# A matrix product with layer norm on one core: four row blocks worked on together over halves of B, another load order, and extra matmuls on zeros

## The chip, the cores and the metric

One Trainium2 chip, of which the kernel uses one core. The metric is the device time in microseconds of one execution. The engines of the core run side by side: TensorE (matmuls and transposes), VectorE, ScalarE, POOL (here it issues the loads) and SyncE (here it issues the stores). The profile names them PE (PEld for TensorE's weight loads), DVE, ACT, POOL and SP.

## The reference

```python
def reference(a, b, gamma, beta, eps):       # a, b: 2048 x 2048 float32
    x = np.matmul(a, b)
    mean = np.mean(x, axis=-1, keepdims=True)
    var = np.var(x, axis=-1, keepdims=True)
    normalized = (x - mean) / np.sqrt(var + eps)
    return (gamma * normalized + beta).astype(np.float32)
```

A row of the product can be normalised only when all of its 2048 columns are there. gamma, beta and eps are inputs like a and b; eps is a plain number.

## The kernel before, in words

**Tiles.** The 2048 rows of A are 16 row blocks of 128 (index `i`, later `p`). The contraction has 16 k tiles of 128 (`kt`). The 2048 columns of the result are four quarters of 512 (`q`); one quarter of a row block fills one PSUM bank. There are eight banks: seven for results (`cps`, line 110) and one for transposes (`tps`, line 74).

**Loads.** POOL issues all loads, which also turn float32 into float16. A row block of A (`emit_a_load`, line 62) is one transfer: 1 MB read, 512 KB written. B is loaded once and stays (`b16`): one transfer per k tile over all 2048 columns (line 95), of the same size. The order on the queue is A 0, A 1, B 0 to 15, A 2, A 3, gamma, beta (lines 81 to 99); later blocks of A follow inside the main loop (line 176), each after a buffer has come free (four buffers, line 47).

**Transposes.** TensorE needs A with the contraction on the partitions. `emit_transposes` (line 70) makes, per row block, two halves of eight 128 x 128 transposes into the one `tps` bank; ScalarE copies each half to `at` (line 78) before the next half may be written.

**Main loop (line 159).** For each row block, for each k tile, four matmuls (one per quarter, `emit_mm`, line 113) add into four banks. The transposes of the next row block stand in the middle. In the last row block the quarters run one after the other. When a quarter is complete, `quarter_done` (line 122) measures it (`bn_stats`, VectorE) and copies it to SBUF (`x`, ScalarE), which frees its bank. `emit_ln_stats` makes mean and 1/sqrt(var + eps); `emit_ln_stt` does the two passes of VectorE over each quarter (`u`, line 147, and `c`, line 151), and SyncE stores half a row block at a time (line 157), the last row block in quarters.

**What sets the order.** The order in the program text is a priority. A planner with its own cost model lays out every engine's queue, and an instruction that it deems ready can be put ahead of one that stands earlier in the text. So in the trace the matmuls of row block 1 are mixed with those of row block 0 while B comes in, until the seven banks are taken. All buffers' waits are put in by the framework. Engines work their queues in order.

Of the kernel before, what the change touches and what calls it, by code (L numbers as in the profile page):

```python
# [10 lines left out]
FP16 = mybir.dt.float16  # L11
AluOp = mybir.AluOpType
# [3 lines left out]
@with_exitstack  # L16
def kernel(
    ctx: ExitStack,
    tc: tile.TileContext,
    a: bass.AP,  # L20
    b: bass.AP,
    gamma: bass.AP,
    beta: bass.AP,
    eps: bass.AP,
    out: bass.AP,
):
    nc = tc.nc
    P = 128
    M, K = a.shape
    K2, N = b.shape  # L30
    assert K == K2
    assert M % P == 0 and K % P == 0 and N % 2048 == 0
    n_mt = M // P
    n_kt = K // P
    NB = 512
    n_nb = N // NB

    if isinstance(eps, bass.AP):
        eps_ap = eps
        eps_val = None  # L40
    else:
        eps_ap = None
        eps_val = float(eps)

    konst = ctx.enter_context(tc.tile_pool(name="konst", bufs=1))
    bpool = ctx.enter_context(tc.tile_pool(name="bpool", bufs=1))
    a16p = ctx.enter_context(tc.tile_pool(name="a16p", bufs=4))
    atp = ctx.enter_context(tc.tile_pool(name="atp", bufs=3))
    xpool = ctx.enter_context(tc.tile_pool(name="xpool", bufs=8))
    upool = ctx.enter_context(tc.tile_pool(name="upool", bufs=4))  # L50
    cpool = ctx.enter_context(tc.tile_pool(name="cpool", bufs=2))
    stat = ctx.enter_context(tc.tile_pool(name="stat", bufs=4))
    psum = ctx.enter_context(tc.tile_pool(name="psum", bufs=1, space=bass.MemoryType.PSUM))

    gamma_b = konst.tile([P, N], FP32)
    beta_b = konst.tile([P, N], FP32)
    eps_t = konst.tile([P, 1], FP32)
    ident = konst.tile([P, P], FP16)

    b16 = bpool.tile([P, n_kt, N], FP16)  # L60

    def emit_a_load(i):
        a16 = a16p.tile([P, K], FP16, tag="a16", name=f"a16_{i}")
        nc.gpsimd.dma_start(a16, a[ts(i, P), :])  # L64
        return a16

    a16_lst = [None] * (n_mt + 2)
    at_lst = [None] * (n_mt + 1)

    def emit_transposes(i):  # L70
        a16 = a16_lst[i]
        at = atp.tile([P, n_kt, P], FP16, tag="at", name=f"at{i}")
        for h in range(2):
            t_ps = psum.tile([P, n_kt // 2, P], FP16, tag="tps", bufs=1,
                             name=f"tps{i}_{h}")
            for j in range(n_kt // 2):
                nc.tensor.transpose(t_ps[:, j, :], a16[:, ts(h * 8 + j, P)], ident)  # L77
            nc.scalar.copy(at[:, ds(h * 8, 8), :], t_ps)  # L78
        return at

    a16_lst[0] = emit_a_load(0)
    a16_lst[1] = emit_a_load(1)
    nc.vector.memset(ident, 0.0)  # L83
    nc.gpsimd.affine_select(  # L84
        out=ident, in_=ident, compare_op=AluOp.not_equal, fill=1.0,
        base=0, pattern=[[-1, P]], channel_multiplier=1,
    )
    if eps_ap is not None:
        nc.sync.dma_start(eps_t, eps_ap.unsqueeze(0).to_broadcast([P, 1]))
    else:  # L90
        nc.vector.memset(eps_t, eps_val)
    at_lst[0] = emit_transposes(0)
    at_lst[1] = emit_transposes(1)
    for kt in range(n_kt):
        nc.gpsimd.dma_start(b16[:, kt, :], b[ts(kt, P), :])  # L95
    a16_lst[2] = emit_a_load(2)
    a16_lst[3] = emit_a_load(3)
    nc.gpsimd.dma_start(gamma_b, gamma.unsqueeze(0).to_broadcast([P, N]))  # L98
    nc.gpsimd.dma_start(beta_b, beta.unsqueeze(0).to_broadcast([P, N]))  # L99

    bnst_l = [None] * n_mt
    c_ps_l = [[None] * n_nb for _ in range(n_mt)]
    x_sb_l = [[None] * n_nb for _ in range(n_mt)]
    rstd_l = [None] * n_mt
    mv_l = [None] * n_mt

    def alloc_q(i, q):
        if bnst_l[i] is None:
            bnst_l[i] = stat.tile([P, n_nb, 6], FP32, tag="bnst", name=f"bnst{i}")
        c_ps_l[i][q] = psum.tile([P, NB], FP32, tag="c_ps", bufs=7,  # L110
                                 name=f"cps_{i}_{q}")

    def emit_mm(i, q, kt):
        nc.tensor.matmul(  # L114
            c_ps_l[i][q],
            at_lst[i][:, kt, :],
            b16[:, kt, ds(q * NB, NB)],
            start=(kt == 0),
            stop=(kt == n_kt - 1),
        )  # L120

    def quarter_done(i, q):
        nc.vector.bn_stats(bnst_l[i][:, q, :], c_ps_l[i][q])  # L123
        x_sb = xpool.tile([P, NB], FP32, tag="x_sb", name=f"x_{i}_{q}")
        nc.scalar.copy(x_sb, c_ps_l[i][q])  # L125
        x_sb_l[i][q] = x_sb

    def emit_ln_stats(i):
        mv = stat.tile([P, 2], FP32, name=f"mv{i}")
        nc.vector.bn_aggr(mv, bnst_l[i])  # L130
        ve = stat.tile([P, 1], FP32, name=f"ve{i}")
        nc.vector.tensor_tensor(ve, mv[:, 1:2], eps_t, AluOp.add)  # L132
        sq = stat.tile([P, 1], FP32, name=f"sq{i}")
        nc.scalar.activation(sq, ve, ActFn.Sqrt)  # L134
        rstd = stat.tile([P, 1], FP32, name=f"rstd{i}")
        nc.vector.reciprocal(rstd, sq)  # L136
        mv_l[i] = mv
        rstd_l[i] = rstd

    def emit_ln_stt(i, split_out=2):  # L140
        mv, rstd = mv_l[i], rstd_l[i]
        c_sb = cpool.tile([P, N], FP32, tag="c_sb", name=f"c{i}")
        nq_per_out = n_nb // split_out
        for q in range(n_nb):
            qs = ds(q * NB, NB)
            u = upool.tile([P, NB], FP32, tag="u", name=f"u_{i}_{q}")
            nc.vector.scalar_tensor_tensor(  # L147
                u, x_sb_l[i][q], mv[:, 0:1], gamma_b[:, qs],
                AluOp.subtract, AluOp.mult,
            )  # L150
            nc.vector.scalar_tensor_tensor(  # L151
                c_sb[:, qs], u, rstd, beta_b[:, qs],
                AluOp.mult, AluOp.add,
            )
            if (q + 1) % nq_per_out == 0:
                o = ds((q + 1 - nq_per_out) * NB, nq_per_out * NB)
                nc.sync.dma_start(out[ts(i, P), o], c_sb[:, o])

    for i in range(n_mt):
        last = i == n_mt - 1  # L160
        for q in range(n_nb):
            alloc_q(i, q)
        if last:
            for q in range(n_nb):
                for kt in range(n_kt):
                    emit_mm(i, q, kt)
                quarter_done(i, q)
        else:
            for kt in range(n_kt):
                for q in range(n_nb):  # L170
                    emit_mm(i, q, kt)
                if kt == n_kt // 2 - 1:
                    if i + 1 >= 3 and i + 1 < n_mt:
                        at_lst[i + 1] = emit_transposes(i + 1)
                    if i + 4 < n_mt:
                        a16_lst[i + 4] = emit_a_load(i + 4)
            for q in range(n_nb):
                if i == 1 and q == 1:
                    at_lst[2] = emit_transposes(2)
                quarter_done(i, q)  # L180
        emit_ln_stats(i)
        if i == 1:
            emit_ln_stt(0)
            emit_ln_stt(1)
        elif i >= 2:
            emit_ln_stt(i, split_out=(2 if not last else 4))


# [33 lines left out]
```

## Time and profile before

| what | us |
|---|---|
| median of four runs (279.56 to 279.72) | 279.65 |
| the profiled execution, whole | 279.64 |
| its span, first to last instruction | 277.6 |
| TensorE matmul and transpose busy | 245.2 |
| VectorE busy | 132.7 |
| ScalarE busy | 74.0 |
| POOL busy | 18.6 |

The span is measured between instructions, so it is shorter than the execution's own time. TensorE's instructions are pipelined: one that is listed with 381 ns may start 0.22 us after the one before it, so the pace is read from the starts of a run of them, and "busy" counts the union of their times. An instruction's line is that of the kernel's text above; several instructions of one line in a row are merged into one row with their count. A wait is put down to what came last by the profile.

### The profile page before, as it was taken

The page shows a single profiled execution, that of the slowest core. Times are in us where ns is not written, and L with a number is a line of the kernel's source. Part 1 is how long each engine was busy: PE and PEld are TensorE (multiplying, and loading weights), DVE is VectorE, ACT ScalarE, POOL GpSimd, SP SyncE. Part 2 cuts the span into 40 slices and gives each one's busy share as a digit, 9 for nine tenths or more (in the row PEclk, how much of TensorE's full clock was granted, in tenths as well). Part 3 has the DMA queues.
Part 4 walks back from the last instruction along what each step waited for, and adds up shares of the span by engine and source line. Part 5 has one row for each costly group of instructions (what it writes and reads, how often), then busy time and mean ns, then how long its engine had stood idle before and what let it go on. Part 6 is the DMA issues. An engine that isn't in the chain of part 4 may idle for free.

```text
span 277.6 us, 3149 instructions
## 1 busy us (share of the span) xinstructions
PE 245.2 (88%) x1280; PEld 116.2 (42%) x1280; DVE 132.7 (48%) x242; ACT 74.0 (27%) x114; POOL 18.6 (7%) x39
## 2 busy tenths in 40 slices
PE   0597657989999999999999999999999999999940
PEld 0252222445454444445454545454444545454410
DVE  0000000489663829091837456372909192745754
ACT  1220000562322222232323232222223232323110
POOL 7222211000000000000000000000000000000000
PEclk9999999999999999999999999999999999999995
DMA  6999999998734251616061433425111203030304
GB/s 114 212 213 212 214 216 210 308 272 235 217 151 78 100 128 76 153 44 178 8 188 39 162 67 151 76 113 116 76 76 64 91 0 153 0 151 2 151 0 151
DMA packets 9805, 35.84 MB, mean 129 GB/s; under 512 B 1088, under 2 KB 1088, under 8 KB 9536
## 3 DMA queue, kind: packets, MB, share of 16 engines
q0 software_dynamic: 4896, 18.88, 33.7%
q1 hardware_dynamic: 4896, 16.78, 15.2%
q8 instruction: 10, 0.16, 0.3%
q14 instruction: 3, 0.02, 0.0%
HBM read 35.65 MB, written 16.78 MB: 189 GB/s over the span
## 4 chain that ended last, share of the span: by engine, by line
PE 78%; DMA 17%; DVE 2%; issue 1%; ACT 1%; DVEq 0%; POOL 0%; ACTq 0%; POOLq 0%
PE cps L114 72%; DMA b<-in_b_dram 14%; PE tps L77 5%; DMA a<-in_a_dram 3%; DVE u L147 1%; ACT at L78 1%; DVE c L151 1%; DVE bnst L123 0%; DVEq L217 0%; POOL a L64 0%; DVE mv L130 0%; DVE ve L132 0%; DVE rstd L136 0%; ACTq L78 0%; POOLq L203 0%
## 5 line engine op out<-in xcount | busy, mean ns | idle before, releaser
L114 PE MATMUL cps<-b,at 128*128 128x512 f16 x1024 | 231.6, 381 | 12.8 <-DMA b<-in_b_dram 12.8
L114 PEld LDWEIGHTS <-at 128*128 128x128 f16 x1024 | 99.3, 98 | 130.5 <-issue 20.4
L123 DVE BATCH_NORM_STATS2 bnst<-cps 128x6 f32<-128x512 f32 x64 | 40.1, 687 | 135.2 <-PE cps L114 135.2
L125 ACT COPY x<-cps 128x512 f32<-128x512 f32 x64 | 37.5, 587 | 106.9 <-DVE bnst L123 106.1
L78 ACT COPY at<-tps 128x1024 f16<-128x1024 f16 x32 | 32.4, 1012 | 86.6 <-PE tps L77 86.6
L147 DVE SCALAR_TENSOR_TENSOR u<-x,mv,gamma_b 128x512 f32<-128x512 f32 x64 | 46.0, 743 | 2.2 <-DMA gamma_b<-in_gamma_dram 2.2
L151 DVE SCALAR_TENSOR_TENSOR c<-u,rstd,beta_b 128x512 f32<-128x512 f32 x64 | 45.2, 747 | 0.0
L77 PE MATMUL tps<-ident,a 128*128 128x128 f16 x256 | 21.1, 230 | 9.0 <-DMA a<-in_a_dram 6.5
L77 PEld LDWEIGHTS <-a 128*128 128x128 f16 x256 | 18.2, 103 | 19.8 <-issue 8.4
L64 POOL DMA_DIRECT2D a<-in_a_dram x16 | 8.6, 537 | 145.8 <-PE tps L77 137.6
L95 POOL DMA_DIRECT2D b<-in_b_dram x16 | 8.5, 542 | 18.1 <-DMA b<-in_b_dram 15.4
L130 DVE BATCH_NORM_AGGREGATE mv<-bnst 128x2 f32<-128x24 f32 x16 | 4.2, 264 | 0.5
L134 ACT ACTIVATE sq<-ve 128x1 f32<-128x1 f32 x16 | 3.3, 206 | 0.2 <-DVE ve L132 0.2
L136 DVE RECIPROCAL rstd<-sq 128x1 f32<-128x1 f32 x16 | 2.5, 158 | 1.7 <-ACT sq L134 1.7
L132 DVE TENSOR_TENSOR ve<-mv,eps_t 128x1 f32<-128x1 f32 x16 | 2.5, 159 | 0.5
L78 ACT ACT_TABLE_LOAD x1 | 1.3, 1283 | 0.7 <-PEq L203 0.7
L134 ACT ACT_TABLE_LOAD x1 | 1.3, 1283 | 0.0
L99 POOL DMA_DIRECT2D beta_b<-in_beta_dram x1 | 0.5, 527 | 3.5 <-DMA b<-in_b_dram 3.5
L98 POOL DMA_DIRECT2D gamma_b<-in_gamma_dram x1 | 0.5, 527 | 1.9 <-DMA b<-in_b_dram 1.9
L83 DVE MEMSET ident<- 128x64 uint32 x1 | 0.1, 112 | 0.8 <-PEq L203 0.8
L84 POOL TENSOR_SCALAR_AFFINE_SELECT ident<-ident 128x128 f16<-128x128 f16 x1 | 0.3, 312 | 0.1
L203 POOL MEMSET const-float32-0.0<- 128x1 f32 x1 | 0.1, 99 | 0.2 <-issue 0.2
(4 smaller groups left out, 0.4 us busy)
## 6 DMA issues: line engine op xcount, KB each, us to landing
out_dram<-c SPq DMA_DIRECT2D x30, 512.0 KB, 2.6
a<-in_a_dram POOLq DMA_DIRECT2D x16, 512.0 KB, 5.2
b<-in_b_dram POOLq DMA_DIRECT2D x16, 512.0 KB, 19.4
gamma_b<-in_gamma_dram POOLq DMA_DIRECT2D x1, 1024.0 KB, 20.3
beta_b<-in_beta_dram POOLq DMA_DIRECT2D x1, 1024.0 KB, 18.8
out_dram<-c SPq DMA_DIRECT2D x4, 256.0 KB, 2.6
```

The source lines that it names most:

```text
L64: nc.gpsimd.dma_start(a16, a[ts(i, P), :])
L77: nc.tensor.transpose(t_ps[:, j, :], a16[:, ts(h * 8 + j, P)], ident)
L78: nc.scalar.copy(at[:, ds(h * 8, 8), :], t_ps)
L95: nc.gpsimd.dma_start(b16[:, kt, :], b[ts(kt, P), :])
L114: nc.tensor.matmul(c_ps_l[i][q], at_lst[i][:, kt, :], b16[:, kt, ds(q * NB, NB)], start=(kt == 0), stop=(kt == n_kt - 1),)
L123: nc.vector.bn_stats(bnst_l[i][:, q, :], c_ps_l[i][q])
L125: nc.scalar.copy(x_sb, c_ps_l[i][q])
L130: nc.vector.bn_aggr(mv, bnst_l[i])
L132: nc.vector.tensor_tensor(ve, mv[:, 1:2], eps_t, AluOp.add)
L134: nc.scalar.activation(sq, ve, ActFn.Sqrt)
L147: nc.vector.scalar_tensor_tensor(u, x_sb_l[i][q], mv[:, 0:1], gamma_b[:, qs], AluOp.subtract, AluOp.mult,)
L151: nc.vector.scalar_tensor_tensor(c_sb[:, qs], u, rstd, beta_b[:, qs], AluOp.mult, AluOp.add,)
```

## The change

Four row blocks (0 to 3) are now worked on together. B is loaded in halves of its columns: first, for every k tile, columns 0 to 1023 (quarters 0 and 1), then for every k tile columns 1024 to 2047. On the first halves TensorE adds into seven quarters at once: (0,0), (0,1), (1,0), (1,1), (2,0), (2,1), (3,0), the list `L7`; then (3,1) alone; then quarters 2 and 3 of row blocks 0 and 1, and then those of 2 and 3. Row blocks 4 to 15 run as before.

On the load queue, row block 0 of A comes in two halves, blocks 1 to 3 stand between the first half tiles of B, and all later blocks are issued behind gamma and beta, each waiting for a free buffer. The transposes of row blocks 4 and 5 stand in the stage of row blocks 2 and 3, and later ones are made two row blocks ahead instead of one. There are six `at` buffers instead of three and 20 `x` buffers instead of eight.

The order of TensorE's instructions in the first stage (up to (3,1)) is written out by hand and kept by `manual_schedule`. In it stand 29 extra matmuls on a tile of zeros (`emit_warm`), in groups of nine, three, two, eight, two, three and two, whose result is overwritten.

```diff
--- before.py
+++ after.py
@@ -34,6 +34,10 @@
     n_kt = K // P
     NB = 512
     n_nb = N // NB
+    NH = N // 2
+
+    n_start = 4
+    assert n_mt > n_start
 
     if isinstance(eps, bass.AP):
         eps_ap = eps
@@ -45,8 +49,8 @@
     konst = ctx.enter_context(tc.tile_pool(name="konst", bufs=1))
     bpool = ctx.enter_context(tc.tile_pool(name="bpool", bufs=1))
     a16p = ctx.enter_context(tc.tile_pool(name="a16p", bufs=4))
-    atp = ctx.enter_context(tc.tile_pool(name="atp", bufs=3))
-    xpool = ctx.enter_context(tc.tile_pool(name="xpool", bufs=8))
+    atp = ctx.enter_context(tc.tile_pool(name="atp", bufs=6))
+    xpool = ctx.enter_context(tc.tile_pool(name="xpool", bufs=20))
     upool = ctx.enter_context(tc.tile_pool(name="upool", bufs=4))
     cpool = ctx.enter_context(tc.tile_pool(name="cpool", bufs=2))
     stat = ctx.enter_context(tc.tile_pool(name="stat", bufs=4))
@@ -59,9 +63,13 @@
 
     b16 = bpool.tile([P, n_kt, N], FP16)
 
-    def emit_a_load(i):
+    def emit_a_load(i, split=False):
         a16 = a16p.tile([P, K], FP16, tag="a16", name=f"a16_{i}")
-        nc.gpsimd.dma_start(a16, a[ts(i, P), :])
+        if split:
+            nc.gpsimd.dma_start(a16[:, 0:NH], a[ts(i, P), 0:NH])
+            nc.gpsimd.dma_start(a16[:, NH:K], a[ts(i, P), NH:K])
+        else:
+            nc.gpsimd.dma_start(a16, a[ts(i, P), :])
         return a16
 
     a16_lst = [None] * (n_mt + 2)
@@ -77,26 +85,6 @@
                 nc.tensor.transpose(t_ps[:, j, :], a16[:, ts(h * 8 + j, P)], ident)
             nc.scalar.copy(at[:, ds(h * 8, 8), :], t_ps)
         return at
-
-    a16_lst[0] = emit_a_load(0)
-    a16_lst[1] = emit_a_load(1)
-    nc.vector.memset(ident, 0.0)
-    nc.gpsimd.affine_select(
-        out=ident, in_=ident, compare_op=AluOp.not_equal, fill=1.0,
-        base=0, pattern=[[-1, P]], channel_multiplier=1,
-    )
-    if eps_ap is not None:
-        nc.sync.dma_start(eps_t, eps_ap.unsqueeze(0).to_broadcast([P, 1]))
-    else:
-        nc.vector.memset(eps_t, eps_val)
-    at_lst[0] = emit_transposes(0)
-    at_lst[1] = emit_transposes(1)
-    for kt in range(n_kt):
-        nc.gpsimd.dma_start(b16[:, kt, :], b[ts(kt, P), :])
-    a16_lst[2] = emit_a_load(2)
-    a16_lst[3] = emit_a_load(3)
-    nc.gpsimd.dma_start(gamma_b, gamma.unsqueeze(0).to_broadcast([P, N]))
-    nc.gpsimd.dma_start(beta_b, beta.unsqueeze(0).to_broadcast([P, N]))
 
     bnst_l = [None] * n_mt
     c_ps_l = [[None] * n_nb for _ in range(n_mt)]
@@ -156,7 +144,117 @@
                 o = ds((q + 1 - nq_per_out) * NB, nq_per_out * NB)
                 nc.sync.dma_start(out[ts(i, P), o], c_sb[:, o])
 
-    for i in range(n_mt):
+    a16_lst[0] = emit_a_load(0, split=True)
+    nc.gpsimd.dma_start(b16[:, 0, 0:NH], b[ts(0, P), 0:NH])
+    nc.vector.memset(ident, 0.0)
+    nc.gpsimd.affine_select(
+        out=ident, in_=ident, compare_op=AluOp.not_equal, fill=1.0,
+        base=0, pattern=[[-1, P]], channel_multiplier=1,
+    )
+    if eps_ap is not None:
+        nc.sync.dma_start(eps_t, eps_ap.unsqueeze(0).to_broadcast([P, 1]))
+    else:
+        nc.vector.memset(eps_t, eps_val)
+    a16_lst[1] = emit_a_load(1)
+    nc.gpsimd.dma_start(b16[:, 1, 0:NH], b[ts(1, P), 0:NH])
+    a16_lst[2] = emit_a_load(2)
+    nc.gpsimd.dma_start(b16[:, 2, 0:NH], b[ts(2, P), 0:NH])
+    a16_lst[3] = emit_a_load(3)
+    for kt in range(3, n_kt):
+        nc.gpsimd.dma_start(b16[:, kt, 0:NH], b[ts(kt, P), 0:NH])
+    for kt in range(n_kt):
+        nc.gpsimd.dma_start(b16[:, kt, NH:N], b[ts(kt, P), NH:N])
+    nc.gpsimd.dma_start(gamma_b, gamma.unsqueeze(0).to_broadcast([P, N]))
+    nc.gpsimd.dma_start(beta_b, beta.unsqueeze(0).to_broadcast([P, N]))
+    a16_lst[4] = emit_a_load(4)
+    a16_lst[5] = emit_a_load(5)
+    for i in range(6, n_mt):
+        a16_lst[i] = emit_a_load(i)
+
+    warm = konst.tile([P, NB], FP16)
+    nc.vector.memset(warm, 0.0)
+    L7 = [(p, q) for p in range(n_start) for q in (0, 1)][:-1]
+    with tc.manual_schedule(engines={mybir.EngineType.PE}):
+        for (p, q) in L7:
+            alloc_q(p, q)
+
+        def emit_warm(n):
+            # times zero, into a bank that row 3's first start=True overwrites
+            for _ in range(n):
+                nc.tensor.matmul(c_ps_l[3][0], warm[:, 0:P], warm, start=True, stop=True)
+
+        def half_tr(i, h):
+            if h == 0:
+                at_lst[i] = atp.tile([P, n_kt, P], FP16, tag="at", name=f"at{i}")
+            t_ps = psum.tile([P, n_kt // 2, P], FP16, tag="tps", bufs=1, name=f"tps{i}_{h}")
+            for j in range(n_kt // 2):
+                nc.tensor.transpose(t_ps[:, j, :], a16_lst[i][:, ts(h * 8 + j, P)], ident)
+            nc.scalar.copy(at_lst[i][:, ds(h * 8, 8), :], t_ps)
+
+        def mm(p, kt):
+            emit_mm(p, 0, kt)
+            if p < 3:
+                emit_mm(p, 1, kt)
+
+        emit_warm(9)
+        half_tr(0, 0)
+        emit_warm(3)
+        half_tr(0, 1)
+        emit_warm(2)
+        mm(0, 0)
+        emit_warm(8)
+        half_tr(1, 0)
+        emit_warm(2)
+        mm(0, 1)
+        half_tr(1, 1)
+        emit_warm(3)
+        mm(1, 0)
+        mm(1, 1)
+        half_tr(2, 0)
+        mm(0, 2)
+        half_tr(2, 1)
+        mm(1, 2)
+        emit_warm(2)
+        mm(2, 0)
+        mm(2, 1)
+        mm(2, 2)
+        half_tr(3, 0)
+        mm(0, 3)
+        mm(1, 3)
+        mm(2, 3)
+        half_tr(3, 1)
+        mm(0, 4)
+        mm(1, 4)
+        mm(2, 4)
+        for kt in range(5):
+            mm(3, kt)
+        for kt in range(5, n_kt):
+            for p in range(n_start):
+                mm(p, kt)
+        for (p, q) in L7:
+            quarter_done(p, q)
+        alloc_q(3, 1)
+        for kt in range(n_kt):
+            emit_mm(3, 1, kt)
+        quarter_done(3, 1)
+
+    for g in range(2):
+        pairs = [(p, q) for p in (2 * g, 2 * g + 1) for q in (2, 3)]
+        for (p, q) in pairs:
+            alloc_q(p, q)
+        for kt in range(n_kt):
+            for (p, q) in pairs:
+                emit_mm(p, q, kt)
+            if g == 1 and kt in (7, 11):
+                at_lst[4 + kt // 11] = emit_transposes(4 + kt // 11)
+        for (p, q) in pairs:
+            quarter_done(p, q)
+        for p in (2 * g, 2 * g + 1):
+            emit_ln_stats(p)
+        for p in (2 * g, 2 * g + 1):
+            emit_ln_stt(p)
+
+    for i in range(n_start, n_mt):
         last = i == n_mt - 1
         for q in range(n_nb):
             alloc_q(i, q)
@@ -170,20 +268,12 @@
                 for q in range(n_nb):
                     emit_mm(i, q, kt)
                 if kt == n_kt // 2 - 1:
-                    if i + 1 >= 3 and i + 1 < n_mt:
-                        at_lst[i + 1] = emit_transposes(i + 1)
-                    if i + 4 < n_mt:
-                        a16_lst[i + 4] = emit_a_load(i + 4)
+                    if i + 2 < n_mt:
+                        at_lst[i + 2] = emit_transposes(i + 2)
             for q in range(n_nb):
-                if i == 1 and q == 1:
-                    at_lst[2] = emit_transposes(2)
                 quarter_done(i, q)
         emit_ln_stats(i)
-        if i == 1:
-            emit_ln_stt(0)
-            emit_ln_stt(1)
-        elif i >= 2:
-            emit_ln_stt(i, split_out=(2 if not last else 4))
+        emit_ln_stt(i, split_out=(2 if not last else 4))
 
 
 # ---- launch: one core; inputs and outputs as the reference has them ----
```

## Rows read from the trace of the kernel before

**Rows 1.** The profile page: the span, and the chain that ended last, by engine.

```profile
span 277.6 us, 3149 instructions
...
PE 78%; DMA 17%; DVE 2%; issue 1%; ACT 1%; DVEq 0%; POOL 0%; ACTq 0%; POOLq 0%
```

**Rows 2.** Who waited for whom: us in total, times, the longest.

```profile
DVE bnst L123 <- PE cps L114: 135.2, 16, 48.7
...
PE cps L114 <- DMA b<-in_b_dram: 12.8, 14, 2.3
...
PE tps L77 <- DMA a<-in_a_dram: 6.5, 1, 6.5
...
PE tps L77 <- ACT at L78: 2.2, 2, 1.1
```

**Rows 3.** Timeline, 0 to 62 us, POOL and TensorE: start, length, instruction, idle before.

```profile
1.24 1.19 POOL L64 DMA_DIRECT2D a<-in_a_dram  x2 [0.79 <-POOLq L203]
...
6.51 1.04 PE L77 MATMUL tps<-ident,a 128*128 128x128 f16 x8 [6.51 <-DMA a<-in_a_dram]
...
15.13 2.34 PE L114 MATMUL cps<-b,at 128*128 128x512 f16 x5
...
18.07 2.35 PE L114 MATMUL cps<-b,at 128*128 128x512 f16 x10
...
36.00 1.67 PE L114 MATMUL cps<-b,at 128*128 128x512 f16 x7 [0.77 <-DMA b<-in_b_dram]
```

**Rows 4.** Stages: stretch, length, busy time by engine, granted clock, DMA share, GB/s.

```profile
6.50:48.50 42.00, 28.82 (x129) 13.21 (x130) 0.00 (x0) 4.05 (x4) 8.45 (x16) 1.00 1.06 213
...
49.20:267.00 217.80, 216.37 (x1151) 103.02 (x1150) 126.05 (x228) 68.01 (x107) 5.28 (x10) 1.00 0.39 115
```

**Rows 5.** The chain in order of time: start, length, what.

```profile
67.38 12.85 PE cps L114 x59
80.23 0.45 PE tps L77 x8
...
81.77 0.61 PE tps L77 x8
...
247.38 19.66 PE cps L114 x91
```

**Rows 6.** Transfers issued between 9 and 36 us.

```profile
b<-in_b_dram POOLq DMA_DIRECT2D x9, 512.0 KB, 20.3
a<-in_a_dram POOLq DMA_DIRECT2D x2, 512.0 KB, 20.4
```

**Rows 7.** Transfers, 92.5 to 97.5 us: packets, MB, share of 16 engines.

```profile
q1 hardware_dynamic: 216, 0.82, 40.7%
```

**Rows 8.** Transfers, 267.5 to 277.6 us: packets, MB, share of 16 engines.

```profile
q1 hardware_dynamic: 576, 1.05, 29.8%
```

**Rows 9.** Loads by source line, L64 (A) above, L95 (B) below.

```profile
DMA to landing us min/median/max: 5.0/5.2/20.4
...
DMA to landing us min/median/max: 8.6/19.4/21.0
```

**Rows 10.** Timeline of VectorE and ScalarE, whole run.

```profile
0.83 0.11 DVE L83 MEMSET ident<- 128x64 uint32 x1 [0.83 <-PEq L203]
...
52.74 1.28 ACT L134 ACT_TABLE_LOAD   x1
...
56.61 0.75 DVE L147 SCALAR_TENSOR_TENSOR u<-x,mv,gamma_b 128x512 f32<-128x512 f32 x1 [2.17 <-DMA gamma_b<-in_gamma_dram]
...
87.60 2.49 DVE L123 BATCH_NORM_STATS2 bnst<-cps 128x6 f32<-128x512 f32 x4 [6.65 <-PE cps L114]
...
94.53 1.41 DVE L151 SCALAR_TENSOR_TENSOR c<-u,rstd,beta_b 128x512 f32<-128x512 f32 x2
...
263.61 0.70 DVE L123 BATCH_NORM_STATS2 bnst<-cps 128x6 f32<-128x512 f32 x1 [1.46 <-PE cps L114]
...
264.39 0.59 ACT L125 COPY x<-cps 128x512 f32<-128x512 f32 x1 [1.57 <-DVE bnst L123]
```

## The prediction

> **What bounds the kernel now.** I read the chain of waits first, because it says whose work makes the end late: TensorE holds 78% of the span, transfers 17%, and no other engine over 2% [rows 1]. The list of who waited for whom names the 17%: TensorE's matmuls waited 12.8 us for tiles of B in 14 waits, its transposes 6.5 us for the first tile of A and 2.2 us for ScalarE's copy [rows 2]. The timeline of TensorE says when: it starts at 6.51, then does seven matmuls per tile of B and waits about 0.8 us for the next [rows 3]; by the stages this ends at 49.2 [rows 4]. Seven, because PSUM holds seven result banks: row block 0 takes four and row block 1 the other three, and nothing else is open until both are done. TensorE is busy 28.8 of the 42 us up to 48.5 and 216.4 of the 217.8 us after 49.2 [rows 4], so only the load stage has anything to give.
>
> The chain in order of time prices the steady stage [rows 5]: 59 matmuls take 12.85 us, 0.218 each, and the two half transposes of a row block 0.45 + 0.61, 0.53 each. A row block is 64 x 0.218 + 2 x 0.53 = 15.0 us. The useful work of the whole kernel at that pace is 1024 x 0.2178 = 223.0 plus 32 x 0.53 = 17.0, or 240.0 us. TensorE ends at 247.38 + 19.66 = 267.04; from the first tile's landing, 6.51 + 240.0 would be 246.5. So 20.5 us are lost: 15.0 in waits [rows 2], the rest mostly in a slow clock. Up to 17.5 us the matmuls stand 0.43 us apart (five in 2.34, the last one drawn longer) and eight transposes take about 1.0; from 18.07 on ten matmuls take 2.35 [rows 3]. 512 columns in 0.43 us is the 1.2 GHz level, in 0.218 the 2.4 GHz level; the granted-clock column reads 1.00 in both, so here the level is read from the spacing. After TensorE's end come 277.6 - 267.0 = 10.6 us of last evacuation, normalisation and store, and the profiled execution is 279.64 us, 2.04 over its span. It equals the median of the four runs (279.65), so the sum is made against it unadjusted.
>
> **The change, part by part.** *B in two column halves, four row blocks on the first half.* Seven banks still, but now (0,0) to (3,0) without (3,1). Per half tile, TensorE again has seven matmuls, 7 x 0.218 = 1.53 us, where the half tile needs about half a tile's transfer. Whole tiles: 11 loads between 9 and 36 us, 2.45 each [rows 6]. A half tile isn't in the trace. From below: half, 1.22. From above, by neighbours: the 512 KB stores with 4 KB rows occupied the 16 engines 40.7% of 5 us for 0.82 MB, 2.04 us or 1.30 per 128 rows [rows 7]; the four 256 KB stores with 2 KB rows 29.8% of 10.1 us, 3.01 or 0.75 each [rows 8]. A half tile reads 4 KB rows, whose neighbour is 1.30, and writes 2 KB rows; priced wholly as 2 KB rows it would be two of 0.75, 1.50. I take 1.25, between half and 1.30, and keep 1.50 for the range.
>
> The Trainium skill's page DMA: Bandwidth & Descriptors (section Rules for kernel authors) asks for at least 1 MiB per transfer, and its table under Bandwidth gives a 1 MB transfer 341 GB/s; by that figure a half tile of 0.52 MB would be 1.54 us, an estimate, and the sum about 6 us higher (13.8 + 32 x 1.54 against 56.9, both worked out below). The trace's 4 KB rows disagree, at 0.82 MB in 2.04 us of full occupation, about 400 GB/s.
>
> *When tiles land.* A tile of A loaded alone lands 5.0 us after issue at best [rows 9], the first of all 5.3 (issue 1.24, landing 6.51) [rows 3]. Its first half lands 1.22 earlier, 5.3 rounded. Behind it on the same queue: its second half, 1.22; three whole tiles of A, 7.35; sixteen first halves of B, 20.0. The last first half lands at 33.8, the last second half 20.0 later, at 53.8; gamma and beta at 56.3 and 58.7, A tiles 4 and 5 at 61.2 and 63.6. POOL issues each in about 0.6 us [rows 3], under 1.25, with about eight in flight (B's loads land 19.4 us after issue, eight times 2.45 [rows 9]), so issuing doesn't bind, and its 17 more issues, 10 us, lie beside the transfers. A tiles 8 to 15 still wait on POOL for a buffer, but only other loads of A stand behind them.
>
> *29 warm matmuls.* On zeros, so they use no loaded data. One memset more on VectorE (the similar one took 0.11 for a quarter of the bytes [rows 10]), so TensorE can start near 1.4: nine at 0.43 end at 5.3, just as A lands, and cost nothing. The other 20 stand in the order and cost 20 x 0.218 = 4.4 us, of which an unknown part would have been waiting anyway; I charge them whole, and count waits only over them.
>
> *The early stretch.* From 5.3 to the end of the five matmuls of row 3 there are 35 matmuls (7.6), 8 half transposes (4.2) and the 20 warm ones (4.4): 16.2 us, 21.5 if nothing waited. From the transfers' side: A tile 3 lands at 17.6 (5.3 + 1.22 + three halves of B + three tiles of A), and behind it stand two halves and 17 matmuls, 4.8, so 22.4 at the earliest. I take 23.5: 2.0 us for waits on both sides and for a clock that is still low for the first two or three microseconds. Low end 0.9. High end: the clock stays at its 1.2 GHz level to 17.5, as now [rows 3]; then half of 12.2 us is lost, 6.1, with 0.5 of waits, 6.6.
>
> The page TensorE: Matmul & The Clock Gate of the Trainium skill says (Part 1: The HAM clock gate) that half rate is the default and sustained matmul activity releases it, but also (Part 4: PE-mode transpose) that transposes don't count as activity in the same way. By the first the nine would do it, by the second the interleaved transposes could undo it. The trace fits either: in its slow stretch, transposes and waits alternate with few matmuls.
>
> *After that.* Eleven k tiles of seven matmuls: 16.8, to 40.3. The last of them needs B's last first half at 38.8; it lands at 33.8, so TensorE binds. Quarter (3,1): 16 matmuls on one bank, which the last row block does at 19.66/91 = 0.216 now [rows 5]; 3.5, to 43.8. It needs the bank of (0,0), whose evacuation (from 263.61 to 264.98 for a like one, 1.4 [rows 10]) has the six matmuls behind it, 1.3, for cover: nothing, up to 0.3. Row blocks 0 and 1 on the second half: 64 matmuls, 13.9, to 57.8, the last k tile needed at 56.9 against 53.8. Row blocks 2 and 3 with the transposes of 4 and 5: 13.9 + 2.1, to 73.9; A tile 4 is used at 64.8 and landed at 61.2. Then 12 row blocks, 167.3, with ten pairs of half transposes, 10.6: TensorE ends at 251.7 or so. The same by the total: 5.3 + 240.0 + 4.4 + 2.0 = 251.7.
>
> *VectorE.* Its normalising work for rows 0 to 3 comes in two blocks. One row block now runs from 87.60 to 95.94, 8.3 us, of which 2.5 is bank statistics [rows 10]. A block of two with four banks still to measure is 2.5 + 2 x 5.9 = 14.2, and 1.3 for the one table load of ScalarE [rows 10]. Rows 0 and 1: 57.8 to 73.3, just before 73.9, when the next banks finish. Rows 2 and 3: 73.9 to 88.1, before row block 4 at 88.9. Cover of 0.6 and 0.8 us: nothing charged, but thin. Beta at 58.7 is ahead of its use near 62; now gamma is what holds this up, by 2.2 us at 56.61 [rows 10].
>
> **Sum.** 251.7 + 10.6 + 2.04 = 264.3. The tail is the same code. What is late next is TensorE itself, with nothing to wait for.
>
> **The rivals.** *Clock late.* The 1.2 GHz level lasts to 17.5 in spite of the warm matmuls: for it the present slow stretch, against it that TensorE would now be in work without a break from 1.4. 6.6 instead of 2.0: 268.9.
>
> *Half tiles dearer, transfers bind the second pass.* The last half lands at 13.8 + 32 h, needed at 56.9: from h = 1.35 on, every 0.1 us costs 3.2. At 1.50, priced as the 2 KB rows, 61.8: 4.9 more, 269.2. For it, written rows shrink to 2 KB; against it the 1.30 of 4 KB rows.
>
> *Slower.* If a load's time goes with its 128 rows and not its bytes, a half costs as much as a whole, 2.45: the last lands at 92.2, 35 us late, 299. It outweighs the gain from h = 1.35 + 15.3/32 = 1.83. Against it: the 2 KB store rows at 0.75 are well under the 1.30 of 4 KB rows, so bytes matter.
>
> *Evacuation late.* VectorE is in order, so if a block of two rows runs over, the next banks aren't freed; three free banks last 0.65 us, and TensorE stands for the rest. With 1.5 us over in each of two blocks: 267.3. For it, cover under 1 us; against it, VectorE waits 135 us for TensorE in all [rows 2].
>
> **How the numbers follow.** Forecast, 263 to 266: 0.62. Clock late: 0.13. Half tiles at 1.35 to 1.7 us: 0.11. Evacuation late: 0.09. Slower, half tiles over 1.83: 0.03. The remaining 0.02 is a gain that vanishes by a mixture. The range runs from 262.0 (waits and slow clock at 0.9, 1.1 less, and a quarter of the warm matmuls lying in waits, 1.2 less) to 269.5, which takes in the prices of the clock, of 1.50 and of evacuation. A measurement of this kernel can tell about 0.2% from no change; faster by more has 0.95, within it 0.01, slower 0.04.
>
> **What would show it.** Matmuls 0.218 us apart from 8 us on or sooner; from 24 to 250 us TensorE with no wait on B; the last second half landing near 54 and k tile 15 of the second pass not waiting on it; TensorE's last matmul near 251.7; the tail still 10.6 long. The prediction is wrong if TensorE waits on B beyond 24 us (half tiles dear), if its spacing is 0.43 beyond 10 (clock), or if it stands waiting for bank copies near 74 and 89 (evacuation).

## The result, and the profile after

The changed kernel takes 265.34 us (median of 8 runs, 265.18 to 265.63) where the kernel before takes 279.64 (13 runs in all); the ratio is 0.949, 95% interval 0.948 to 0.950. The forecast was 264.3. The profiled execution is 265.18 us.

The page after: the span, and the chain that ended last by engine. Transfers held 17% of the chain [rows 1] and hold 5% now.

```profile
span 263.3 us, 3209 instructions
...
PE 88%; DMA 5%; DVE 2%; POOL 1%; ACT 1%; issue 1%; DVEq 0%; POOLq 0%; ACTq 0%
```

Who waited for whom, after. The matmuls' waits for B went from 12.8 us in 14 waits [rows 2] to 1.8 in three, the transposes' waits for A from 6.5 to 0.3: the nine matmuls on zeros now stand where that first wait was.

```profile
DVE bnst L111 <- PE cps L102: 124.3, 17, 39.1
...
PE cps L102 <- DMA b<-in_b_dram: 1.8, 3, 0.7
...
PE tps L191 <- ACT at L192: 0.4, 1, 0.4
...
PE tps L191 <- DMA a<-in_a_dram: 0.3, 2, 0.2
```

The stages after (stretch, length, busy time of PE, PEld, DVE, ACT and POOL, clock, DMA share, GB/s). In the load stage TensorE was busy 28.8 of 42 us [rows 4]; from 24 to 58 us it now is 33.9 of 34.0, while transfers run as hard as before.

```profile
9.00:24.00 15.00, 13.37 (x95) 7.10 (x95) 0.00 (x0) 6.32 (x7) 4.34 (x9) 1.00 1.08 208
24.00:41.80 17.80, 17.69 (x83) 7.95 (x82) 1.44 (x3) 0.69 (x2) 7.32 (x15) 1.00 1.12 207
41.80:58.00 16.20, 16.20 (x76) 7.35 (x76) 3.55 (x6) 4.00 (x7) 5.75 (x11) 1.00 1.10 254
```

The start of TensorE's timeline after; L184 are the matmuls on zeros, L191 the transposes, L102 the matmuls. The first k tile's matmuls stand at 9.32, the last wait for B ends at 17.06, and the row at 22.46 begins with the last eleven matmuls of the early stretch.

```profile
1.27 4.02 PE L184 MATMUL cps<-warm 128*128 128x512 f16 x9 [1.27 <-DVE warm L175]
5.45 1.04 PE L191 MATMUL tps<-ident,a 128*128 128x128 f16 x8 [0.16 <-DMA a<-in_a_dram]
...
7.59 0.61 PE L191 MATMUL tps<-ident,a 128*128 128x128 f16 x8 [0.38 <-ACT at L192]
...
9.32 0.59 PE L102 MATMUL cps<-b,at 128*128 128x512 f16 x2 [0.69 <-DMA b<-in_b_dram]
...
11.80 0.62 PE L191 MATMUL tps<-ident,a 128*128 128x128 f16 x8 [0.17 <-DMA a<-in_a_dram]
...
13.30 0.59 PE L102 MATMUL cps<-b,at 128*128 128x512 f16 x2 [0.45 <-DMA b<-in_b_dram]
...
17.06 0.59 PE L102 MATMUL cps<-b,at 128*128 128x512 f16 x2 [0.67 <-DMA b<-in_b_dram]
...
22.46 7.72 PE L102 MATMUL cps<-b,at 128*128 128x512 f16 x35
```

The chain in order of time after (start, length, what). The one break between 22.63 and 66 us is the evacuation of bank (0,0) before quarter (3,1): 0.71 and 0.59, of which all but 0.1 to 0.3 lies beside the six matmuls behind it.

```profile
22.63 17.71 PE cps L102 x82
...
40.36 0.71 DVE bnst L111
...
41.09 0.59 ACT x L113
...
41.73 24.39 PE cps L102 x112
...
219.18 33.58 PE cps L102 x155
```

### The profile page after: what moved, and what is told of

It is laid out like the page before. It is cut to its first block, busy times and chain, and to the rows that moved or that the text cites. A ratio compares the mean times of both kernels' runs of the same rounds, so it can differ in the third digit from the quotient of the medians.

```text
span 263.3 us, 3209 instructions
## 1 busy us (share of the span) xinstructions
PE 248.5 (94%) x1309; PEld 117.7 (45%) x1309; DVE 132.3 (50%) x243; ACT 74.4 (28%) x114; POOL 27.5 (10%) x56
## 4 chain that ended last, share of the span: by engine, by line
PE 88%; DMA 5%; DVE 2%; POOL 1%; ACT 1%; issue 1%; DVEq 0%; POOLq 0%; ACTq 0%
PE cps L102 83%; PE tps L85 5%; DMA b<-in_b_dram 5%; DVE u L135 1%; ACT at L86 1%; DVE c L139 1%; DVE bnst L111 1%; PE tps L191 1%; POOL a L72 0%; DVEq L307 0%; POOL a L69 0%; ACT x L113 0%; POOL b L148 0%; POOL b L159 0%; PE cps L184 0%
## 5 line engine op out<-in xcount | busy, mean ns | idle before, releaser
L102 PE MATMUL cps<-b,at 128*128 128x512 f16 x1024 | 227.4, 379 | 2.0 <-DMA b<-in_b_dram 1.8
L102 PEld LDWEIGHTS <-at 128*128 128x128 f16 x1024 | 99.0, 98 | 118.0 <-issue 5.4
L85 PEld LDWEIGHTS <-a 128*128 128x128 f16 x192 | 12.7, 97 | 8.0 <-issue 3.7
L85 PE MATMUL tps<-ident,a 128*128 128x128 f16 x192 | 14.6, 219 | 0.4
L184 PE MATMUL cps<-warm 128*128 128x512 f16 x29 | 9.4, 461 | 1.3 <-DVE warm L175 1.3
L166 POOL DMA_DIRECT2D b<-in_b_dram x16 | 8.4, 528 | 12.0 <-DMA b<-in_b_dram 12.0
L164 POOL DMA_DIRECT2D b<-in_b_dram x13 | 6.9, 533 | 14.0 <-DMA b<-in_b_dram 7.6
L191 PEld LDWEIGHTS <-a 128*128 128x128 f16 x64 | 4.3, 103 | 3.8 <-DMA a<-in_a_dram 2.1
L191 PE MATMUL tps<-ident,a 128*128 128x128 f16 x64 | 5.3, 231 | 0.7 <-ACT at L192 0.4
L184 PEld LDWEIGHTS <-warm 128*128 128x128 f16 x29 | 3.1, 115 | 4.7 <-issue 2.1
```

What stands on the lines that cost most here:

```text
L102: nc.tensor.matmul(c_ps_l[i][q], at_lst[i][:, kt, :], b16[:, kt, ds(q * NB, NB)], start=(kt == 0), stop=(kt == n_kt - 1),)
L166: nc.gpsimd.dma_start(b16[:, kt, NH:N], b[ts(kt, P), NH:N])
L184: nc.tensor.matmul(c_ps_l[3][0], warm[:, 0:P], warm, start=True, stop=True)
L191: nc.tensor.transpose(t_ps[:, j, :], a16_lst[i][:, ts(h * 8 + j, P)], ident)
```

## The experiments

Eleven kernels, each timed against the kernel before on the same chip (279.6 to 279.7 each time). Times are medians; those of 264 and 265 us have ranges of 0.2 to 0.9 us, given where a difference rests on them.

**e4: whole tiles of B.** The halves undone, all else kept.

```diff
-        nc.gpsimd.dma_start(b16[:, kt, 0:NH], b[ts(kt, P), 0:NH])
+        nc.gpsimd.dma_start(b16[:, kt, :], b[ts(kt, P), :])
...
-    for kt in range(n_kt):
-        nc.gpsimd.dma_start(b16[:, kt, NH:N], b[ts(kt, P), NH:N])
```

> B loaded by whole k tiles in the same place of the queue; TensorE's order, the four row blocks, the load order of A and the matmuls on zeros kept. Theory (the gain comes from seven matmuls per half tile instead of seven per whole tile): the last tile lands at 53 to 55, (3,1) and all second halves come after it, TensorE ends at 266 to 268, 279 to 280.5 in all: the whole gain is gone. Rival (the gain comes from an earlier start, the clock and the early loads of A): at most half of it goes, 265 to 272.

Measured: 280.44 us, ratio to before 1.003 (1.002 to 1.004). The whole gain is gone, and TensorE ends at 267.60 as the theory had it. Its waits for B are much like those of the kernel before [rows 2], and so is the picture of seven matmuls and a wait per tile; here from its timeline, up to the last tile:

```profile
PE cps L102 <- DMA b<-in_b_dram: 13.8, 13, 2.2
```

```profile
49.94 1.67 PE L102 MATMUL cps<-b,at 128*128 128x512 f16 x7 [0.86 <-DMA b<-in_b_dram]
52.37 1.67 PE L102 MATMUL cps<-b,at 128*128 128x512 f16 x7 [0.77 <-DMA b<-in_b_dram]
54.79 26.18 PE L102 MATMUL cps<-b,at 128*128 128x512 f16 x119 [0.74 <-DMA b<-in_b_dram]
```

Four row blocks, the early loads of A, the hand-written order and the matmuls on zeros, together but without the halves, are worth nothing. The halves without the four row blocks were not run, so the gain is shown for the two together.

**e5: the kernel before with the nine matmuls on zeros at its start.**

```diff
+    for _ in range(9):
+        nc.tensor.matmul(w_ps, warm[:, 0:P], warm, start=True, stop=True)
     at_lst[0] = emit_transposes(0)
```

> The kernel before with nothing but the nine matmuls on zeros put at its start. Theory (in the load stage transfers set the pace, seven matmuls per whole tile at either level of the clock): 279.6, unchanged within 0.3. Rival (the slow clock's 4 us at the start are lost time): 276 to 278.

Measured: 279.58 against 279.72, ratio 0.9995 (0.9987 to 1.0004): no change. The clock wasn't even lifted: transposes and matmuls behind the nine still go at the 1.2 GHz level (eight transposes 1.03, four matmuls 1.86), so this run says nothing of what a lifted clock would have brought, and for the kernel before no run does.

```profile
6.41 1.03 PE L77 MATMUL tps<-ident,a 128*128 128x128 f16 x8 [1.11 <-DMA a<-in_a_dram]
...
11.32 1.86 PE L119 MATMUL cps<-b,at 128*128 128x512 f16 x4 [1.76 <-DMA b<-in_b_dram]
```

**e1: no matmuls on zeros; e2: only the first nine.** One number in `emit_warm`:

```diff
-            for _ in range(n):
+            for _ in range(0):                      # e1
+            for _ in range(9 if n == 9 else 0):     # e2
```

> All 29 matmuls on zeros left out, nothing else. Theory (they lift the clock, and lie in waits anyway): the matmuls stay 0.43 us apart until about 18 us or later, but TensorE still waits for transfers till 17 us, so the loss is only what is slow behind that: 0.5 to 2 us, 265.8 to 267.3. Rival 1 (the clock rises by itself, they only cost time): 264.9, faster by the two that stand behind the last wait, 0.4 us. Rival 2 (sparse work never lifts the clock during the load stage): low level until about 40 us, 275 or more.

> The first nine matmuls on zeros kept, the other 20 left out. Theory A (once lifted, the clock stays up through waits of under 1 us): the other 20 lay in waits but for two, 264.9. Theory B (with so little to do between 7 and 17 us the clock falls back): as without any, 265.8 to 267.3, and matmuls 0.43 us apart again after 9 us.

Measured: e1 265.12 us (265.06 to 265.43), e2 264.59 (264.54 to 264.75). Without any, the clock is at its 1.2 GHz level until 16 us, and the end hardly moves: TensorE ends at 252.87, against 252.76.

```profile
9.08 1.01 PE L102 MATMUL cps<-b,at 128*128 128x512 f16 x2 [0.45 <-DMA b<-in_b_dram]
...
14.54 1.91 PE L102 MATMUL cps<-b,at 128*128 128x512 f16 x4
...
18.22 0.61 PE L191 MATMUL tps<-ident,a 128*128 128x128 f16 x8 [0.67 <-ACT at L192]
```

With nine, theory B's clock came true, and a time near theory A's: up at 5.49 (eight transposes in 0.62), down again at 8.88 (two matmuls in 1.01; the granted clock is 0.53 from 8.8 to 15 us), up by 15.68. And yet it is 0.75 us faster than the changed kernel.

```profile
5.49 0.62 PE L191 MATMUL tps<-ident,a 128*128 128x128 f16 x8 [0.58 <-DMA a<-in_a_dram]
...
8.88 1.01 PE L102 MATMUL cps<-b,at 128*128 128x512 f16 x2 [1.06 <-DMA b<-in_b_dram]
...
15.68 0.61 PE L191 MATMUL tps<-ident,a 128*128 128x128 f16 x8 [0.15 <-ACT at L192]
```

That is not the price of the other 20. The loads landed sooner in these two traces, though they are issued in the same order: POOL's issue that follows the landing of B's half tile 2 stands at 17.30 in the changed kernel, at 16.86 in e1 and at 16.61 in e2 (rows in this order). Whether the matmuls on zeros hold the loads up, or something else does, wasn't separated.

```profile
17.30 0.53 POOL L164 DMA_DIRECT2D b<-in_b_dram  x1 [0.77 <-DMA b<-in_b_dram]
16.86 0.53 POOL L164 DMA_DIRECT2D b<-in_b_dram  x1 [0.70 <-DMA b<-in_b_dram]
16.61 0.53 POOL L164 DMA_DIRECT2D b<-in_b_dram  x1 [0.73 <-DMA b<-in_b_dram]
```

Of the 20, the two behind the last wait for B stand on the changed kernel's chain, 0.43 us; the others lie in waits.

```profile
18.53 0.43 PE cps L184 x2
```

In e1 the last load on the chain is the one before 12.88, and behind it stand slow work and a copy of ScalarE's:

```profile
12.88 1.01 PE cps L102 x2
...
14.75 1.71 PE cps L102 x4
...
17.15 1.02 ACT at L192
```

So an estimate of what the low clock costs there, from these numbers: e1 has its loads 0.44 us earlier, saves 0.43 and yet ends 0.11 later, 1.0 us in all. For e2 it is 0.69 + 0.43 less 0.64 (TensorE ends at 252.12), 0.5 us. The 20 matmuls are about even with that, and the gain of e2 is as large as its earlier loads.

**e3: the first row block of A in one transfer; e7: that and only nine matmuls on zeros.**

```diff
-    a16_lst[0] = emit_a_load(0, split=True)
+    a16_lst[0] = emit_a_load(0)
```

> The first row block of A loaded by one transfer instead of two halves. Theory (splitting the first transfers sets the 16 queues apart, and that is why B's first half tile landed at 9.3 instead of 7.7): A lands at 6.6, B's first half tile at 7.9, everything behind it 1.4 us earlier, TensorE's early waits shrink: 264.3. Rival (half tiles among the first transfers do it, split or not, or the queue simply starts slowly): B's first half tile again near 9.3, and the first transposes 1.1 us later lie in that wait: 265.3.

> First row block of A in one transfer and only the first nine matmuls on zeros. Theory (with earlier landings the other 20 lie on the path, not in waits): both gains add in part, 264.0. Rival (both took the same waiting away): 264.5, as either alone. If the clock's fall costs more now that work comes sooner: 265.

Measured: e3 264.52 us (264.02 to 264.89), e7 264.30 (264.20 to 264.36). The first transposes of e3 start 0.9 us later, B's first half tile is there before it is asked for, and the last wait for B ends at 15.91 instead of 17.06. Rows of e3:

```profile
6.35 0.62 PE L191 MATMUL tps<-ident,a 128*128 128x128 f16 x8 [1.05 <-DMA a<-in_a_dram]
...
8.94 0.59 PE L102 MATMUL cps<-b,at 128*128 128x512 f16 x2
...
15.91 0.59 PE L102 MATMUL cps<-b,at 128*128 128x512 f16 x2 [0.53 <-DMA b<-in_b_dram]
```

Against the changed kernel the undivided first transfer gives 0.8 us; with nine matmuls on zeros in both (e7 against e2) it gives 0.3, and the ranges are apart. e7 lies between its theory and its rival. Its range lies inside that of e3, so what the 20 matmuls cost or give isn't clear there. In these two traces the loads land alike (POOL's issue as above at 16.15 and 16.14), and TensorE ends at 251.64 in e3 and at 252.02 in e7, which had the clock low again from 12.69 to about 16 us.

**e6: A's first four row blocks in halves of their columns; e8: the same with another order.** In e6 the first halves stand between B's first half tiles, the second halves behind its half tile 5; TensorE's order follows. Behind the first nine, eight matmuls on zeros are left in e6 and six in e8, instead of 20. In e8 the second halves stand behind half tile 3, and at least six matmuls are put between a half transpose and the matmul that reads its copy.

```diff
+    a_half(0, 0); a_half(1, 0); b_half(0, 0); a_half(2, 0); b_half(1, 0); a_half(3, 0)
+    for kt in range(2, 6):          # e8: (2, 3)
+        b_half(kt, 0)
+    for p in range(4):
+        a_half(p, 1)
+        b_half(6 + p, 0)            # e8: 4 + p
```

> The changed kernel with the first four row blocks of A loaded in halves of their columns: the four first halves between B's first two half tiles, the second halves behind B's half tiles 5 to 8, and TensorE's first stage in that order; eight matmuls on zeros in later places instead of 20. Theory (the early stretch is bound by the 4 MB of A ahead of and between B's first half tiles): row 3 joins 6 us sooner, about 2.5 us of early waiting go, then B's last half tile, landing at 56.5 to 57, binds the second pass: 263.5. If the smaller transfers also set the queues apart as in the changed kernel, up to 264.5. Rival (the order of A is not what binds): 265.3.

> The kernel with A's first four row blocks in halves, with the second halves two half tiles earlier on the queue and TensorE's first stage re-ordered so that at least six matmuls stand between a half transpose and the first matmul that reads its copy. Theory (e6 lost 3.3 us to ScalarE's copies, and behind them the last half tile of B at 57 binds): those waits go, the first pass ends near 39.5 instead of 40.7, the second pass ends with the last half tile at 57.9 instead of 58.3: 264.2 to 264.5, with waits on B back at the end of the second pass. Rival (transfers don't bind there): 263.4.

Measured: e6 264.78 us (264.40 to 264.99), e8 264.24 (264.01 to 264.31). e6 missed its 263.5: it waits 3.3 us for ScalarE's copies, in an order that left nothing between a transpose and its reader. Its waits:

```profile
PE cps L102 <- ACT at L204: 2.2, 2, 1.1
...
PE tps L203 <- ACT at L204: 1.1, 1, 1.1
```

e8 has none of these, and is where the theory put it: now the last half tile binds. Its chain goes back through B's queue from the end of the second pass, which in the changed kernel it doesn't:

```profile
46.97 10.18 DMA b<-in_b_dram
...
57.19 7.99 PE cps L102 x36
```

**e9, e10, e11: the second pass over six quarters.** Row blocks 0 to 2 together, then row block 3; e9 on top of e8, e10 on top of e7, e11 as e9 with VectorE's normalising put later.

```diff
-    for g in range(2):
-        pairs = [(p, q) for p in (2 * g, 2 * g + 1) for q in (2, 3)]
+    six = [(p, q) for p in range(3) for q in (2, 3)]
```

> As e8_a_k_order, and the second pass over six quarters (row blocks 0 to 2, then row block 3 by quarters) instead of twice four. Theory (as above: the last half tile binds a pass of four matmuls per half tile, not one of six): no wait on B in the second pass, TensorE ends at 250.7, 263.3. Rival (VectorE, with three row blocks to normalise at once, frees the banks too late): TensorE stands near 80, 264 to 266.

> As e7_a0_whole_nine, with the second pass over six quarters. Theory (in e7 TensorE never waited for B in the second pass, so this part gives nothing by itself): 264.3. Rival (VectorE late): 265 to 266.

> As e9_a_k_order_six, but with VectorE's normalising of row blocks 1 to 3 placed behind the statistics of row block 3's last two quarters, and row block 3's behind row block 4's; the transposes of 4 and 5 a little later. Theory (e9 and e10 lost 3 us because banks waited behind three row blocks of normalising on VectorE's queue, nothing else): TensorE's stall at 93 us goes from 1.5 to under 1, ScalarE's waits go, 263.3 to 264.5. Rival (the pass over six quarters costs elsewhere, in TensorE's order): 266.5 or more.

Measured: 267.35 (266.57 to 269.57), 266.98 (266.69 to 267.04) and 266.12 us (265.86 to 269.3). Two of e9's six times and one of e11's lie 2 to 3 us above the others, and no run says why; the traces are of others. The rival of e9 and e10 holds in its mechanism, at a price above the one it named: VectorE, with nothing to normalise until 64 us and three row blocks after that, reaches the two quarters of row block 3 at 80 us and row block 4's only at 93, and TensorE stands 1.5 us for a bank, and 1.6 for ScalarE's copies. From the timeline of e9's VectorE, and its waits:

```profile
78.68 1.41 DVE L139 SCALAR_TENSOR_TENSOR c<-u,rstd,beta_b 128x512 f32<-128x512 f32 x2
80.01 1.29 DVE L111 BATCH_NORM_STATS2 bnst<-cps 128x6 f32<-128x512 f32 x2
...
93.17 2.48 DVE L111 BATCH_NORM_STATS2 bnst<-cps 128x6 f32<-128x512 f32 x4
```

```profile
PE tps L85 <- ACT at L86: 1.6, 2, 1.0
PE cps L102 <- ACT x L113: 1.5, 1, 1.5
```

e11 shortens the stall to 0.9 us and leaves 1.4 us of waiting for ScalarE's copies: 266.1, neither the 263.3 to 264.5 of its theory nor wholly its rival's. How much of the rest is the pass itself wasn't separated.

No version beats the changed kernel by much; the best, e8, by 1.1 us (0.4%), ratio to before 0.945 (0.944 to 0.946), and e7 is level with it.

## Why the prediction was right, step by step

**The mechanism holds.** Seven matmuls per half tile instead of seven per whole tile is the whole gain: e4 gives it all back. The clock rose in time: from 7.59 on (eight transposes in 0.61) no matmul of the changed kernel was slow. What was said to happen from 24 us on did: no wait on B, (3,1) delayed by about 0.3, the second pass and the rest at 0.218 per matmul, 15.0 per row block, a tail of 10.5.

**The term that was mis-sized: waits and slow clock in the early stretch,** 2.0 us in the sum. The early stretch ended at 24.85 (22.46 and eleven matmuls of 0.216) instead of 23.5, so the term is 24.85 - 5.3 - 16.2 = 3.3 us. Of this, 2.4 us are the waits in the rows from 5.45 to 17.06 (0.38, 0.69, 0.17, 0.45 and 0.67); the rest, 0.9, is in the main slow work up to 7.59 and a start at 5.45 instead of 5.3. That is the miss: TensorE ended at 252.76 instead of 251.7, and what comes behind it took 265.18 - 252.76 = 12.4 instead of 12.6. The low and high ends of the term, 0.9 and 6.6, held it.

Its cause is in the landing times, which the prediction had summed from a first landing and a steady spacing. A's first half landed on time, 5.45. B's first half tile did not: 9.32 instead of 7.8, and everything behind it stayed 1.5 to 2 us late. POOL's issues after show landings, because each waits for the load eight places ahead of it and follows its landing by about 0.24 us (9.56 here, 9.32 on TensorE): A's second half landed near 6.8, B's first half tile at 9.3.

```profile
7.03 0.53 POOL L164 DMA_DIRECT2D b<-in_b_dram  x1 [0.55 <-DMA a<-in_a_dram]
9.56 0.53 POOL L164 DMA_DIRECT2D b<-in_b_dram  x1 [2.00 <-DMA b<-in_b_dram]
12.04 0.53 POOL L164 DMA_DIRECT2D b<-in_b_dram  x1 [1.95 <-DMA a<-in_a_dram]
```

That one half tile took 2.5 us behind its predecessor; by the same reading it took 1.9 to 2.3 in e1, e2, e3, e6, e7 and e8, never 1.25. With A's first row block undivided (e3), B's half tile 2 lands 1.15 us sooner than in the changed kernel, but only 0.5 to 0.7 sooner than in e2 and e1, which keep the split: so the split is 0.5 to 1.15 us of the lateness. Why the first half tile takes about 2 us and later ones 1.28 isn't settled.

**A half tile at 1.25 us:** sixteen second halves are issued from 27.6 to 46.8, 1.28 apart, and land 9.9 us after issue. So the last lands at 56.7, not 53.8: 1.5 to 2 us from the late start, and 0.03 on each of 32.

```profile
L166 POOL DMA_DIRECT2D b<-in_b_dram x16: 527/527/530, 27.6 to 46.8; - x16
...
DMA to landing us min/median/max: 9.7/9.9/10.2
```

It is needed at 58.3 (41.73 and 76 matmuls), so the cover was 1.6 us where the prediction had 3.1; e8, which starts the second pass sooner, runs out of it. The bound of 1.50 from 2 KB rows was far off. The Trainium skill's table (DMA: Bandwidth & Descriptors, Bandwidth) gives 341 GB/s for 1 MB, which made the estimate 1.54 us. It doesn't fit loads with eight in flight: 1.28 us for 0.52 MB read is 410 GB/s, where whole tiles of 1.05 MB in 2.45 us had 428.

**The rival of the slow clock** was given 268.9 on the premise that TensorE's own work binds up to 17.5 us. That price was too high: e1 keeps the clock low until 16 us and loses about 1.0 us by the estimate above. Until 12.88 TensorE waits for transfers there, and slow work lies in those waits; only what is slow behind that is on the path. Of the 4.4 us charged for 20 of the matmuls on zeros, the 0.43 of the last two is on the chain; the rest lies in waits.

That activity lifts the clock and idleness lowers it, the Trainium skill has in TensorE: Matmul & The Clock Gate, Part 1. e2 agrees: up behind nine matmuls in a row, down behind waits of 0.58, 1.10 and 1.06 us. Nine alone did not lift it in e5. The same part puts the price of the ramp under 1% of a kernel. The 1.0 us of e1 is 0.4%.

**The rival of late evacuation** stayed away in the changed kernel, with more cover than the 0.6 and 0.8 us that were worked out: VectorE's first block ran from 58.55 to 73.4 and then waited 1.15 us for TensorE, the second from 74.57 to 88.2, with 1.36 us. The rows after, each with the wait ahead of it:

```profile
74.57 2.49 DVE L111 BATCH_NORM_STATS2 bnst<-cps 128x6 f32<-128x512 f32 x4 [1.15 <-PE cps L102]
...
89.57 2.49 DVE L111 BATCH_NORM_STATS2 bnst<-cps 128x6 f32<-128x512 f32 x4 [1.36 <-PE cps L102]
```

e9 and e10 show how thin that is: with three row blocks in one go the time is 2.7 us (e10 against e7) to 3.1 us (e9 against e8) longer. The wait for a bank, which the rival means, is 1.3 and 1.5 us of it; ScalarE's late copies are 1.6 in both.

## What to carry to other kernels

While a load stage binds, count the matmuls that each transfer sets free against its time, and cut the operand so that the ratio goes up; here half of B's columns for twice the rows does it, and nothing else in the change that was tried matters beside it. Work at a slow clock, and work added to lift it, are free only as long as the next tile is late, so price both by what stands behind the last wait. When the transfers' total no longer binds, the first few landings do: take those from a trace. Splitting the very first one cost 0.3 to 0.8 us here. And before a small gain is put down to an edit, look whether the loads landed alike in both traces.

## What the runs showed of the hardware that was not expected

Among the first transfers a half tile took 2.5 us behind its predecessor (landing 6.8 to 9.3), and 1.9 to 2.3 in six other versions, against 1.28 later. Loads issued in the same order landed up to 0.7 us apart (the changed kernel, e1 and e2). Nine matmuls in a row left TensorE at its 2.4 GHz level in e2, e3 and e7 (the next eight transposes took 0.62, after waits of 0.58, 1.05 and 1.12 us), but at the 1.2 GHz level in e5 and in the changed kernel's own trace (1.03 and 1.04, after 1.11 and 0.16). With sparse work the level fell again in e2 by 8.88 us, after waits of 1.1 us or less; in e8, with waits of 1.1 us or less and six more matmuls on zeros between them, it stayed at 2.4 GHz.
